# A transformer block on one core: value products, modulation sums, routing of expert 0 and the last experts rearranged

## The chip, the cores and the metric

The kernel runs on one core of one Trainium2 chip, written in Bass and Tile. The metric is the device time of one execution in microseconds; the time before is the median of three runs, 1007.59 us (1006.1 to 1008.08). Lower is better.

## What is computed

One encoder block over 1024 tokens of width 1024, all in 32-bit floats. The reference, cut to what matters here:

```
sh1, sc1, g1, sh2, sc2, g2 = split(silu(c) @ w_ada + b_ada, 6)     # modulation, six rows of 1024
h = rmsnorm(x, norm_mix_g) * (1 + sc1) + sh1
u_f, q, k, v = split(h @ w_in, [512, 1024, 1152])                   # 512 Fourier, 8 query heads, 2 key/value heads of 64
q, k = rmsnorm(q, q_norm_g), rmsnorm(k, k_norm_g)
y_f = fourier_mix(u_f, w_fourier, b_fourier)
y_a = windowed_gqa(q, k, v, rel_bias, sink)                         # 128-token blocks, window of +-128
x = x + g1 * (concat(y_f, y_a) @ w_out)
h2 = rmsnorm(x, norm_ffn_g) * (1 + sc2) + sh2
aff = softmax(h2 @ w_router)                                        # 16 experts
for each expert: the 128 tokens with the largest aff; x[token] += g2 * aff * (silu(t @ w_gate) * (t @ w_up)) @ w_down
```

## The kernel before, in words

The tokens are eight tiles of 128. The work has four stages that follow each other on TensorE.

**Mixing stage (lines 200 to 544).** Tiles 0 and 1 are projected together while w_in is split into a high and a low part (three products stand for one 32-bit product). In this part the order on every engine is the written one: `in_order` (line 132) chains each engine's instructions. Then a loop over tiles 2 to 7 takes each in two halves (`for m, (t, kc0)`, line 500). A half transposes and splits the next chunk (`chunk`, line 265: TensorE transposes, ScalarE evacuates with scale and bias and makes the high part, VectorE the low part) and runs four `project` steps of nine products each. At a tile's first half x of tile t+3 is loaded, that of t+1 is scaled on ScalarE (`scale_x`, line 228) and that of t+2 is normalised (`norm_x`, line 225: ScalarE squares, VectorE, a power on GpSimd). After each `project` step comes `bg_tick` (line 358). It moves on the key and query normalisations of finished tiles (`qknorm`, line 285, a generator whose `yield`s count ticks: squares and a power; two ticks later GpSimd's multiplications; some ticks later TensorE's key transposes, line 309) and the modulation rows (`ada_parts`, line 147: VectorE sums eight weighted rows for each of four parts, lines 121 and 123, TensorE sums over the partitions, line 181, VectorE adds a bias, GpSimd stores the row). At every second step the modulation generator is moved on once more (line 537). In this loop no order is pinned: the scheduler of the language orders each engine's instructions by its own estimate of when they are ready.

**Fourier and attention stage (lines 547 to 1026).** For each of 16 units (a tile and a key/value head) `front` makes logits and softmax, and `back` (line 706) transposes the probabilities of two or three key blocks (`flip_p`, ScalarE copies them to a tile pT, two buffers) and multiplies each block with its values (line 727: two products of 64 output rows, side by side in TensorE's columns, two records each). Before, `back` alternates: block b+1 is transposed, `tick` lets other work in, block b is multiplied. `tick` (line 958) hands out steps of a filler: the Fourier part for the first units, then `oproj` (line 760), the output projection, which also writes x2 (the residual), h2 (the normalised rows for the experts) and, through `tail` (line 829), the router's logits and `aff` of each tile. A sorter (`srt`) keeps the best affinities of the first six tiles sorted. The order is the scheduler's.

**Routing (lines 1030 to 1309).** For expert 0 `choose` (line 1138) settles quickly which tokens it takes: it counts, against the sorted best values of six tiles, the affinities of the last two tiles, finds the threshold and ranks. `gate_parts` (line 1106) splits affinities into three bf16 parts. `gather_a` makes one-hot rows from the ranks, `gather` (line 1245) sums token numbers and gates on TensorE (line 1250) and issues GpSimd's indirect load of the chosen rows from h2 in DRAM (line 1259). Then the rows are transposed (line 1306) into xf, and the first six weight units are multiplied as plain 32-bit products (line 1228). `cut_unit` splits a weight unit in two parts (ScalarE high, VectorE low). From `gather(0)` on TensorE, VectorE and GpSimd run in written order (line 1326).

**Experts (lines 1329 to 1357).** Sixteen experts, 192 weight units of 1 MB, streamed through 13 buffers; order pinned on all engines. `put` (line 1273) makes an expert's last products, scales the result by gate and g2 (ScalarE and then GpSimd; for expert 15 one VectorE step, line 1286) and scatters it with an indirect, accumulating DMA (line 1287). All experts write the result into one buffer, ys.

The handling of the last tile decides how the attention stage runs into the routing:

```
normed(slice(0, 512), cur)               # h2 = x2 * rs * G2 (line 805), then + sh2 (line 806)
yield from tail(t, 1)                    # flips of the second half, logits (line 837), aff
normed(slice(512, D), after["aff"])
```

## Time and profile before

| | before |
|---|---|
| median of three runs | 1007.59 us (1006.1 to 1008.08) |
| profiled execution | 1009.72 us |
| its span, first to last instruction | 1007.6 us |
| TensorE busy in it | 949.8 us (94%) |
| VectorE, ScalarE, GpSimd busy | 788.1, 627.8, 404.7 us |
| mean granted TensorE clock | 0.971 |
| mixing stage ends, first product of the experts | about 172 us, 429.54 us |

All times come from one profiled execution, counted from its first instruction. A line such as L309 is a line of the kernel; where a helper records the operation (L81 to L83 for the three products of a split one, L86 and L87 for the split), the tile's name tells which it is. PE is TensorE, DVE VectorE, ACT ScalarE, POOL GpSimd, SP the engine that issues most DMAs. A 32-bit product leaves two records on TensorE. An "idle before" stands with the instruction that ended it, and the arrow names what that one had waited for. The granted clock is a share of TensorE's full clock; it has two levels, 0.50 and 1.00, and a mean between them tells how a stretch divides.

### The profile page before, as it was taken

Reading aid. Unit: us, or ns where it says so; the run is one execution under the profiler, and the core shown is the slowest. Engines: PE = TensorE matmul, PEld = TensorE weight load, DVE = VectorE, ACT = ScalarE, POOL = GpSimd, SP = SyncE. Lnnn points to the kernel's source line nnn. Section 1 sums busy time; section 2 is a strip of 40 time slices with the busy share of each in tenths; the row PEclk is TensorE's granted clock in tenths of the full one; section 3 lists DMA queues with packets and bytes.
Section 4 is the critical chain, followed back from the end, with each engine's and each line's share of the span. In section 5 each row is a group of like instructions: output and inputs, shape, how many; then the busy total and the mean of one; then the engine's idle time right before and its main releaser. Section 6 shows DMA issues by size and latency. Waiting matters only on the chain.

```text
span 1007.6 us, 13138 instructions
## 1 busy us (share of the span) xinstructions
PE 949.8 (94%) x4737; PEld 747.4 (74%) x4737; DVE 788.1 (78%) x1240; ACT 627.8 (62%) x832; POOL 404.7 (40%) x236
## 2 busy tenths in 40 slices
PE   4997999979999999499899999999999999999995
PEld 2675877657777778358788888888888888888884
DVE  1346874787667787879869889988988898899894
ACT  2473533656555552136767777778777777777872
POOL 0025552200000000000257678769766976882203
PEclk9998999989999999599989999999999999999998
DMA  9967582461222228799989999999999999999912
GB/s 291 328 246 251 209 313 83 134 183 47 98 84 74 74 84 289 314 335 355 390 343 359 385 396 399 387 385 409 388 389 385 411 385 389 404 392 387 386 68 42
DMA packets 91641, 283.95 MB, mean 282 GB/s; under 512 B 8140, under 2 KB 25728, under 8 KB 91448
## 3 DMA queue, kind: packets, MB, share of 16 engines
q1 hardware_dynamic: 86712, 266.32, 69.5%
q0 software_dynamic: 4864, 16.80, 6.5%
q8 instruction: 37, 0.61, 0.2%
q14 instruction: 28, 0.23, 0.1%
HBM read 263.79 MB, written 21.40 MB: 283 GB/s over the span
## 4 chain that ended last, share of the span: by engine, by line
PE 83%; DVE 6%; POOL 3%; issue 2%; ACT 2%; DMA 1%; SPq 1%; POOLq 0%; ACTq 0%
PE pa L81 17%; PE pa L82 16%; PE pa L83 16%; PE pu L374 5%; PE yp L727 3%; PE pt L1269 3%; PE pj L81 2%; PE pj L82 2%; PE pt L714 2%; PE pj L83 2%; PE pa L1228 2%; PE pt L837 2%; PE lg L685 1%; DVE ws L123 1%; PE lg L686 1%
## 5 line engine op out<-in xcount | busy, mean ns | idle before, releaser
L87 DVE TENSOR_TENSOR wl<-raw,wh 128x2048 fp32r<-128x2048 f32 (+1 forms) x189 | 424.2, 2275 | 56.0 <-ACT wh L86 54.9
L86 ACT ACTIVATE wh<-raw 128x2048 fp32r<-128x2048 f32 (+1 forms) x189 | 355.4, 1896 | 73.7 <-PE pa L82 65.8
L1242 POOL TENSOR_SCALAR oneh<-tri_f,pos 128x128 bf16<-128x128 f32 x96 | 210.5, 2207 | 15.1 <-PE pt L1250 14.8
L81 PE MATMUL pa<-wh,t1h 128*128 128x512 f32 x384 | 151.4, 394 | 0.0
L83 PE MATMUL pa<-wl,t1h 128*128 128x512 f32 x384 | 149.5, 389 | 0.0
L82 PE MATMUL pa<-wh,t1l 128*128 128x512 f32 x384 | 149.5, 389 | 0.0
L81 PE MATMUL pa<-wh,t0h 128*128 128x512 f32 x360 | 143.5, 399 | 0.0
L82 PE MATMUL pa<-wh,t0l 128*128 128x512 f32 x360 | 141.1, 392 | 0.0
L83 PE MATMUL pa<-wl,t0h 128*128 128x512 f32 x360 | 141.1, 392 | 0.0
L800 POOL TENSOR_TENSOR rs<-ss,mhalf 128x1 f32<-128x1 f32 x8 | 4.5, 558 | 221.3 <-DVE ss L798 194.4
L1284 POOL TENSOR_TENSOR ys<-ys,g_r 128x512 f32<-128x512 f32 x30 | 54.5, 1837 | 84.9 <-ACT ys L1283 84.9
L83 PEld LDWEIGHTS pa<-wl,t1h 128*128 128x128 f32 x384 | 72.1, 188 | 15.1
L82 PEld LDWEIGHTS pa<-wh,t1l 128*128 128x128 f32 x384 | 72.2, 188 | 14.2
L81 PEld LDWEIGHTS pa<-wh,t1h 128*128 128x128 f32 x384 | 72.1, 188 | 14.2
L83 PEld LDWEIGHTS pa<-wl,t0h 128*128 128x128 f32 x360 | 68.1, 189 | 14.5
L81 PEld LDWEIGHTS pa<-wh,t0h 128*128 128x128 f32 x360 | 68.3, 190 | 13.7 <-issue 0.2
L82 PEld LDWEIGHTS pa<-wh,t0l 128*128 128x128 f32 x360 | 68.2, 190 | 13.6 <-issue 0.2
L1259 POOL DMA_INDIRECT xe<-h2d,idx x16 | 18.7, 1171 | 147.3 <-DVE gt L1256 147.2
L1287 POOL DMA_INDIRECT out_dram<-ys,idx x16 | 50.8, 3174 | 10.9 <-DVE ys L1286 6.4
L688 DVE CUSTOM_DVE_ANT_0 sb<-lg,bias,sink 128x384 f32<-128x384 f32 (+1 forms) x64 | 35.3, 579 | 17.4 <-PE pt L714 9.8
L278 ACT ACTIVATE hf<-pt,sh1c,G1c 128x128 f32<-128x128 f32 (+1 forms) x56 | 22.6, 480 | 38.7 <-PE pt L271 38.7
L374 PE MATMUL pu<-wh,hh 128*128 128x512 f32 x128 | 43.6, 423 | 2.3 <-ACT hh L86 2.2
(311 smaller groups left out, 1649.0 us busy)
## 6 DMA issues: line engine op xcount, KB each, us to landing
raw<-in_w_gate_dram SPq DMA_DIRECT2D x64, 1024.0 KB, 10.0
raw<-in_w_up_dram SPq DMA_DIRECT2D x64, 1024.0 KB, 8.5
raw<-in_w_down_dram SPq DMA_DIRECT2D x63, 1024.0 KB, 8.6
raw<-in_w_ada_dram SPq DMA_DIRECT2D x16, 1024.0 KB, 8.6
raw<-in_w_ada_dram SPq DMA_DIRECT2D x16, 512.0 KB, 8.7
xt<-in_x_dram SPq DMA_DIRECT2D x8, 512.0 KB, 5.0
raw<-in_w_out_dram SPq DMA_DIRECT2D x4, 1024.0 KB
raw<-in_x_dram SPq DMA_DIRECT2D x8, 512.0 KB
```

What stands on the lines that cost most here:

```text
L81: PE.matmul(o, lh, rh, start=start, stop=False)
L82: PE.matmul(o, ll, rh, start=False, stop=False)
L83: return PE.matmul(o, lh, rl, start=False, stop=stop)
L86: ACT.activation(hi, src, AF.Copy)
L87: return (eng or DVE).tensor_tensor(lo, src, hi.bitcast(F32), op=OP.subtract)
L374: PE.matmul(acc[:, :c1 - c0], lhs, r[kc][:, c0:c1], start=first, stop=(kc == 7 and r is w_l), skip_group_check=c0 == 1024)
L688: DVE.tensor_tensor_reduce(sb[:, :wid], lg[:, :wid], bias[:, kv * 4 + i, j0:j0 + wid], 1.0, sk[:, i:i + 1], op0=OP.add, op1=OP.max, accum_ ...
L727: PE.matmul(yp[par * 64:par * 64 + 64, :256], vf[:, b, kv * 64:kv * 64 + 64], pT[:, par * 256:par * 256 + 256], start=(bi == 0), stop=(bi ...
L1242: (POOL if t < shared else DVE).tensor_scalar(oneh[:, t, :], slots, pos[:, t, e:e + 1], None, op0=OP.is_equal)
L1269: PE.transpose(p[:, k * 128:k * 128 + 128], src[:, (4 * b + k) * 128:(4 * b + k + 1) * 128], ident)
L1284: POOL.tensor_tensor(ys[:, cs_], ys[:, cs_], g2_r[:, cs_], op=OP.mult)
L1287: POOL.indirect_dma_start(out=out2, out_offset=bass.IndirectOffsetOnAxis(ap=idx[:, :1], axis=0), in_=ys, in_offset=None, compute_op=OP.add)
```

## The change

Mixing stage: the loop's order is pinned on VectorE, ScalarE and GpSimd; x of tile 4 is loaded before the loop; the extra step of the modulation generator goes, so that its sums are spread over the whole loop; tile 1's normalisation starts four ticks later, and key transposes come six ticks after GpSimd's multiplications in place of four. Attention: all blocks of a unit are transposed first, and the value products then stand in one row; pT has three buffers, and one Fourier tile shares the buffer of the Fourier weights. Last tile: h2 is first made as x2 * G2 behind the residual, and then finished by one step per half, the first after aff, the second inside `choose(0)`; the first half's logits stand ahead of the second half's flips. Routing: the last two tiles' gate parts move to GpSimd, ahead of the choice; one equality count moves behind the threshold test; the indirect load is issued before the gate is summed; expert 1's choice and one-hot rows move ahead of the weight splits; the first rows are transposed in groups of 2, 2 and 4. Experts: the last two are scaled on VectorE, and expert 15 writes into the buffer hs in place of ys.

```diff
@@ -31,7 +31,7 @@
 SCRATCH = 4096
-SB, PB, WB, YB = 9, 2, 4, 3
+SB, PB, WB, YB = 9, 3, 4, 3
 OLD = NT - 2
@@ -283,6 +283,10 @@
     def qknorm(t, kk):
+        if t == 1:
+            for _ in range(4):
+                yield
         q_n = qn[t]
@@ -300,10 +304,8 @@
             POOL.tensor_tensor(kd[:, :, dup, :], kv_, gg[:, None, :].to_broadcast([128, 2, 64]), op=OP.mult)
-        yield
-        yield
-        yield
-        yield
+        for _ in range(6):
+            yield
         p = px_[0]()
@@ -459,6 +461,7 @@
     norm_x(3)
+    load_x(4)
     project(pair, 6, hs.pop(6), 0)
@@ -497,6 +500,7 @@
     seq = [(t, kc) for t in range(2, NT) for kc in (0, 4)]
+    t1 = traced()
     for m, (t, kc0) in enumerate(seq):
@@ -507,8 +511,6 @@
         if kc0 == 0:
-            if t == 2:
-                load_x(4)
             if t + 3 < NT:
@@ -533,14 +535,13 @@
                 level0(a)
-            if m > 0 and a % 2:
-                next(ada[0], None)
         if kc0 == 4:
...
         next(g)
+    in_order(t1, "DVE", "Activation", "Pool")
     p_a.close()
@@ -561,7 +562,7 @@
         SP.dma_start(cs, t_in["k_cs"].rearrange("a p c -> p a c"))
-        wf = pf.tile([128, 4, 128], F32, name="wf")
+        wf = pf.tile([128, 4, 128], F32, name="wf", tag="wf", bufs=1)
         POOL.memset(wf, 0.0)
@@ -592,7 +593,7 @@
             ACT.activation(AB[:, i], p.rearrange("p (a b) -> p a b", b=128), AF.Copy)
-        p2 = [pf.tile([128, 2, 256], F32, name=f"p2{i}") for i in range(2)]
+        p2 = [pf.tile([128, 2, 256], F32, name=f"p2{i}", tag=("wf", "p2")[i], bufs=1) for i in range(2)]
         for o in p2:
@@ -716,16 +717,16 @@
-        nxt = flip_p(0)
+        pTs = []
+        for bi in range(len(blocks)):
+            pTs.append(flip_p(bi))
+            yield
+            tick()
         for bi, b in enumerate(blocks):
-            yield
-            pT = nxt
-            if bi + 1 < len(blocks):
-                nxt = flip_p(bi + 1)
-            tick()
             for par in range(2):
                 PE.matmul(yp[par * 64:par * 64 + 64, :256], vf[:, b, kv * 64:kv * 64 + 64],
-                          pT[:, par * 256:par * 256 + 256], start=(bi == 0), stop=(bi == len(blocks) - 1))
+                          pTs[bi][:, par * 256:par * 256 + 256], start=(bi == 0), stop=(bi == len(blocks) - 1))
         ypv = yp[:, :256].rearrange("p (a b) -> p a b", b=128)
@@ -789,6 +790,8 @@
             lastadd = DVE.tensor_tensor(x2[:, cs_], x2[:, cs_], h2[:, cs_], op=OP.add)
+            if t == NT - 1:
+                DVE.tensor_tensor(h2[:, cs_], x2[:, cs_], G2_r[:, cs_], op=OP.mult)
             junk = at0.tile([128, 512], BF, name="junk", tag="qn1")
@@ -808,9 +811,14 @@
                 drain(srt)
-            normed(slice(0, 512), cur)
             yield from tail(t, 1)
-            normed(slice(512, D), after["aff"])
+            def scaled(c, prev):
+                with tc.issue_after(prev.ins):
+                    DVE.scalar_tensor_tensor(h2[:, c], h2[:, c], rs, sh2_r[:, c], op0=OP.mult, op1=OP.add)
+            scaled(slice(0, 512), after["aff"])
+            after["kept"] = lambda kept: scaled(slice(512, D), kept)
         else:
@@ -828,12 +836,17 @@
         x2, rs = x2s.pop(t)
+        p = None
         for b in range(b0, 2):
+            if b0:
+                p = pt()
+                for kc in range(4):
+                    PE.matmul(p[:, :16], x2Ts[t][:, kc, :], wrG[:, kc, :], start=(kc == 0), stop=False)
             x2_flip(t, b, x2)
...
         x2T = x2Ts.pop(t)
-        p = pt()
-        for kc in range(8):
+        p = p or pt()
+        for kc in range(4 * b0, 8):
             PE.matmul(p[:, :16], x2T[:, kc, :], wrG[:, kc, :], start=(kc == 0), stop=(kc == 7))
@@ -1103,12 +1116,12 @@
-    def gate_parts(a, b):
-        DVE.tensor_copy(aux[:, a:b, :, 2], aff[:, a:b])
-        DVE.tensor_tensor(r1[:, a:b], aff[:, a:b], aux[:, a:b, :, 2], op=OP.subtract)
-        DVE.tensor_copy(aux[:, a:b, :, 3], r1[:, a:b])
-        DVE.tensor_tensor(r1[:, a:b], r1[:, a:b], aux[:, a:b, :, 3], op=OP.subtract)
-        DVE.tensor_copy(aux[:, a:b, :, 4], r1[:, a:b])
+    def gate_parts(a, b, eng):
+        eng.tensor_copy(aux[:, a:b, :, 2], aff[:, a:b])
+        eng.tensor_tensor(r1[:, a:b], aff[:, a:b], aux[:, a:b, :, 2], op=OP.subtract)
+        eng.tensor_copy(aux[:, a:b, :, 3], r1[:, a:b])
+        eng.tensor_tensor(r1[:, a:b], r1[:, a:b], aux[:, a:b, :, 3], op=OP.subtract)
+        eng.tensor_copy(aux[:, a:b, :, 4], r1[:, a:b])
@@ -1131,7 +1144,7 @@
         DVE.tensor_tensor(gq[:, :nt], aff[:, :nt, es], th, op=OP.is_gt)
-        DVE.tensor_tensor(gq[:, nt:], aff[:, :nt, es], th, op=OP.is_equal)
+        after["gq"] = DVE.tensor_tensor(gq[:, nt:], aff[:, :nt, es], th, op=OP.is_equal)
         return gq
@@ -1150,6 +1163,7 @@
         k0 = DVE.tensor_scalar(kept, acc[:, 0:1], rank0, 127.0, op0=OP.add, op1=OP.is_le)
+        after.pop("kept", lambda kept: None)(k0)
         with tc.issue_after(k0.ins):
@@ -1157,16 +1171,21 @@
         e0 = DVE.scalar_tensor_tensor(edge, pn[:, :1], rank1, best[:, e:e + 1], op0=OP.is_equal, op1=OP.mult)
+        def equal(a, val, w, wid):
+            junk = rt.tile([128, 256], BF, name="junk", bufs=2)
+            DVE.scalar_tensor_tensor(junk[:, :wid], p[:, :wid], val, w, op0=OP.is_equal, op1=OP.mult,
+                                     accum_out=acc[:, a:a + 1])
         with tc.issue_after(e0.ins):
             above(3, v7)
-            for a, val, w, wid in ((2, v6, below, 128), (4, v7, both, 256)):
-                junk = rt.tile([128, 256], BF, name="junk", bufs=2)
-                DVE.scalar_tensor_tensor(junk[:, :wid], p[:, :wid], val, w, op0=OP.is_equal, op1=OP.mult,
-                                         accum_out=acc[:, a:a + 1])
+            equal(2, v6, below, 128)
         yield
...
         gq = at_least(pe[:, :1], OLD, slice(e, e + 1))
+        with tc.issue_after(after["gq"].ins):
+            equal(4, v7, both, 256)
         yield
@@ -1198,15 +1217,17 @@
-    gate_parts(0, OLD)
+    gate_parts(0, OLD, DVE)
     for m in LATER:
...
     tsp = traced()
+    gate_parts(OLD, NT, POOL)
+    c0 = choose(0)
+    next(c0)
     SP.dma_start(h2d[rows, :], h2)
     SP.dma_start(out2[rows, :], x2)
-    drain(choose(0))
-    gate_parts(OLD, NT)
+    drain(c0)
@@ -1250,14 +1271,14 @@
         DVE.tensor_scalar(idx, p[:, 0:1], p[:, 1:2], None, op0=OP.add)
+        xe = wk.tile([128, D], F32, name="xe", bufs=1)
+        after["p"] = POOL.indirect_dma_start(out=xe, out_offset=None, in_=h2d,
+                                in_offset=bass.IndirectOffsetOnAxis(ap=idx[:, :1], axis=0))
         ax = wk.tile([128, 6], F32, name="ax", bufs=2)
...
         after["v"] = DVE.tensor_tensor(gt[:, 1:2], gt[:, 0:1], ax[:, 2:3], op=OP.add)
-        xe = wk.tile([128, D], F32, name="xe", bufs=1)
-        after["p"] = POOL.indirect_dma_start(out=xe, out_offset=None, in_=h2d,
-                                in_offset=bass.IndirectOffsetOnAxis(ap=idx[:, :1], axis=0))
         gs[e] = idx, gt[:, 1:2], xe
@@ -1276,10 +1297,10 @@
         idx, gate, _ = gs[e]
-        ys = wk.tile([128, D], F32, name="ys", bufs=1)
+        ys = wk.tile([128, D], F32, name="ys" if e < NE - 1 else "hs", bufs=1)
         for hf in range(2):
             cs_ = slice(hf * 512, hf * 512 + 512)
-            if e < NE - 1:
+            if e < NE - 2:
                 ACT.activation(ys[:, cs_], o[hf], AF.Copy, scale=gate)
@@ -1293,19 +1314,16 @@
     SP.dma_start(g2_r, md[3:4, :].to_broadcast([128, D]))
+    drain(choose(1))
+    oneh = gather_a(1)
     cut_unit(2)
-    c1 = choose(1)
-    next(c1)
-    next(c1)
     cut_unit(2)
-    drain(c1)
     xf = wk.tile([128, D], F32, name="ys", bufs=1).rearrange("p (k c) -> p k c", c=128)
-    for b in range(2):
+    for k0, n in ((0, 2), (2, 2), (4, 4)):
         p = pt()
-        for k in range(4):
-            PE.transpose(p[:, k * 128:k * 128 + 128], gs[0][2][:, (4 * b + k) * 128:(4 * b + k + 1) * 128], ident)
-        ACT.activation(xf[:, 4 * b:4 * b + 4], p.rearrange("p (a b) -> p a b", b=128), AF.Copy)
-    oneh = gather_a(1)
+        for k in range(n):
+            PE.transpose(p[:, k * 128:k * 128 + 128], gs[0][2][:, (k0 + k) * 128:(k0 + k + 1) * 128], ident)
+        ACT.activation(xf[:, k0:k0 + n], p[:, :n * 128].rearrange("p (a b) -> p a b", b=128), AF.Copy)
     xh, xl = (wk.tile([128, 8, 128], F32R, name=f"t0{x}", bufs=1) for x in "hl")
```

## Rows read from the trace of the kernel before

**Rows 1.** Waits of TensorE: who waited for whom, us in total, times, longest.

```profile
PE pt L309 <- ACT hf L278: 6.2, 1, 6.2
...
PE pt L1250 <- DVE t1l L87: 3.6, 1, 3.6
```

**Rows 2.** Windows: length, busy time (instructions) of each engine, granted clock, DMA share, GB/s.

```profile
91.40:96.40 5.00, 4.99 (x14) 3.39 (x16) 2.08 (x4) 1.45 (x4) 0.00 (x0) 0.50 0.89 364
...
100.00:116.30 16.30, 16.20 (x87) 12.90 (x86) 13.43 (x16) 8.28 (x19) 10.14 (x11) 1.00 0.50 183
...
223.00:404.00 181.00, 180.60 (x1024) 133.31 (x1023) 135.14 (x472) 97.68 (x268) 4.53 (x9) 0.99 0.30 108
...
404.40:429.50 25.10, 12.13 (x75) 9.94 (x74) 21.18 (x90) 4.07 (x8) 2.36 (x3) 0.55 0.80 314
...
425.00:450.00 25.00, 22.56 (x75) 11.18 (x75) 19.36 (x74) 8.22 (x8) 0.96 (x1) 0.88 0.92 343
```

**Rows 3.** Timeline of GpSimd and ScalarE, 86 to 88 us: start, length, operation.

```profile
86.13 1.53 POOL L196 TENSOR_TENSOR xr<-xs,mhalf 128x1 f32<-128x1 f32 x1
...
87.70 1.15 ACT L229 ACTIVATE xt<-xt,xr 128x1024 f32<-128x1024 f32 x1 [8.79 <-POOL xr L196]
```

**Rows 4.** The instructions of line L123: count, duration min/median/max, first and last start.

```profile
L123 DVE SCALAR_TENSOR_TENSOR ws<-raw,c_act,ws x28: 1269/1285/1418, 75.8 to 141.7; 128x1024 f32<-128x1024 f32 x28
```

**Rows 5.** Timeline of TensorE in the attention stage.

```profile
249.85 0.40 PE L82 MATMUL pj<-woh,yl 128*128 128x512 f32 x1
250.08 0.40 PE L83 MATMUL pj<-wol,yh 128*128 128x512 f32 x1
250.41 0.65 PE L727 MATMUL yp<-pT,vf 128*64 128x256 f32 x4
250.99 0.66 PE L714 MATMUL pt<-ident,sb 128*128 128x128 f32 x4
...
375.09 1.08 PE L727 MATMUL yp<-pT,vf 128*64 128x256 f32 x8
```

**Rows 6.** Windows of line L727 alone: PE and PEld busy (records), clock, DMA.

```profile
223.00:404.00 181.00, 29.49 (x168) 8.97 (x168) 0.99 0.30 108
```

**Rows 7.** Timeline of TensorE in the routing.

```profile
407.33 3.43 PE L837 MATMUL pt<-wrG,x2T 128*128 128x16 f32 x16
...
427.75 1.95 PE L1306 MATMUL pt<-ident,xe 128*128 128x128 f32 x8
429.54 2.63 PE L1228 MATMUL pa<-raw,ys 128*128 128x512 f32 x4
```

**Rows 8.** Timeline of ScalarE in the routing.

```profile
407.57 0.60 ACT L827 ACTIVATE x2T<-pt 128x512 f32<-128x512 f32 x1
```

**Rows 9.** Timeline of VectorE in the routing.

```profile
410.95 0.68 DVE L806 TENSOR_TENSOR raw<-raw,sh_r 128x512 f32<-128x512 f32 x1
...
413.91 0.69 DVE L806 TENSOR_TENSOR raw<-raw,sh_r 128x512 f32<-128x512 f32 x1
...
415.84 0.48 DVE L1164 SCALAR_TENSOR_TENSOR junk<-pt,aff,tri_f 128x256 bf16<-128x256 f32 x1
...
419.76 0.22 DVE L1252 TENSOR_SCALAR idx<-pt 128x1 int32<-128x1 f32 x1 [0.28 <-PE pt L1250]
...
420.36 2.35 DVE L87 TENSOR_TENSOR wl<-raw,wh 128x1024 fp32r<-128x1024 f32 x2
```

**Rows 10.** Timeline of GpSimd in the routing.

```profile
420.83 1.72 POOL L1259 DMA_INDIRECT xe<-h2d,idx  x1 [11.98 <-DVE gt L1256]
```

**Rows 11.** DMA issues, 420 to 424 us: operation, count, median us to landing.

```profile
xe<-h2d,idx POOLq DMA_INDIRECT x1, 5.0
```

**Rows 12.** Timeline of VectorE at the end.

```profile
988.19 4.10 DVE L87 TENSOR_TENSOR wl<-raw,wh 128x1024 fp32r<-128x1024 f32 x2 [0.37 <-ACT wh L86]
998.27 1.41 DVE L1286 SCALAR_TENSOR_TENSOR ys<-pa,gt,g_r 128x512 f32<-128x512 f32 x2 [5.98 <-DMA out_dram<-ys,idx]
```

**Rows 13.** Timeline of TensorE at the end.

```profile
996.97 0.39 PE L83 MATMUL pa<-wl,t1h 128*128 128x512 f32 x1
```

## The prediction

> **What bounds the kernel now.** I read the waits of TensorE first, then windows around the longest of them, then the timelines of the engines that end them, and last the tail. TensorE sets the pace: in the attention and output-projection stretch it is busy 180.60 of 181 us [rows 2], so a microsecond taken out of its own work there is a microsecond off the span, while VectorE, ScalarE and GpSimd matter only where TensorE stands still. It stands still in few places. The longest wait is 6.2 us in the projection loop, before a key transpose (L309); another is 3.6 us at L1250 [rows 1]. The routing stretch from 404.40 to 429.50 has TensorE busy 12.13 of 25.10 us at a mean granted clock of 0.55 [rows 2]: there a chain that hops between TensorE, VectorE, ScalarE and GpSimd sets the time. After the 6.2 us wait the granted clock is 0.50, the lower of its two levels (1.2 GHz), for 5.00 us in which TensorE is busy 4.99 [rows 2], so that work took about 2.5 us longer than at full clock.
>
> **Mixing loop: spread sums, earlier load, pinned order.** The 6.2 us wait ends with ScalarE's chunk evacuation, but ScalarE had itself sat 8.79 us idle until the scaling of tile 4's x at 87.70, and that waited for GpSimd's power for tile 4, run at 86.13 behind the key and query normalisation of tiles 0 and 1 [rows 3]. The change attacks this in three ways: tile 4's x is loaded before the loop (one 512 KB load, ahead of the bias and norm-gain loads and the first w_ada fetches on SP), so that in the written order, now pinned, its power stands ahead of that normalisation; tile 1's normalisation starts four ticks later; and transposes come two ticks later. All 6.2 us can go, and with the wait the half-clock stretch: 6.2 + 2.5 = 8.7 us. What is late next is the modulation sums. There are 28 accumulating steps of 1.285 us (median) [rows 4], plus one plain first step in each of four parts. They now come one per tick instead of one and a half, so VectorE has less per tile: it was busy 13.43 us in a 16.30 us stretch as long as a tile [rows 2], and two steps fewer make about 10.9. But VectorE, ScalarE and GpSimd now run strictly in written order, so VectorE stands still at each chunk's split until ScalarE is through, and TensorE's four column sums (L181) may meet a late accumulator. I set 1.2 us aside for them, a step's length, and take 7.5. Bounds: 0 (another wait takes its place) to 8.7. The shared buffer of the Fourier weights and one spread tile costs nothing: the first write into the tile already follows the products that read the weights. The load costs nothing either, since the loop reads tile 4 only two tiles later; were that cover gone, ScalarE's wait would stay and with it the whole term.
>
> **Value products in one row.** An output-projection product takes 0.23 us from start to start (249.85 to 250.08); the one before a group of value products takes 0.33 (to 250.41), and the group of four records (two products) 0.58 (to 250.99): 0.10 + 0.58 = 0.68 us. A group of eight records that happens to run in one row is 1.08 us long, where four are 0.65, so a block added to a row costs 0.43 [rows 5]. Each merge saves 0.25 us. There are 168 records in this stretch [rows 6], 42 groups, and the 15 units left here become 15 rows: 27 merges, 6.7 us. TensorE's order isn't pinned here, and a product whose operand is ready early may be issued before the others, so I count three quarters, 5.1; bounds 1.5 to 6.7. The third pT buffer only lets the three blocks of a row live together.
>
> **Routing chain.** (a) The 16 records of the last tile's logits run from 407.33 for 3.43 us, 0.214 each [rows 7]. The first eight now run in the idle time before the last flips; the second eight need the copy that ends at 408.17 [rows 8] and end 1.71 later, at 409.9 in place of 410.8: 0.9. (b) The addition at 410.95 (0.68) leaves the path between logits and maximum: 0.5. (c) That at 413.91 (0.69) leaves the path to expert 0's first count: 0.6. (d) In their place one scaled step follows that count, ahead of the edge: -0.7. (e) The equality count at 415.84 (0.48) moves behind the threshold test: 0.35, as a product of TensorE runs under part of it [rows 9]. (f) Five small gate steps leave VectorE's end of the chain: 0.2. On GpSimd they take between 1.1 (0.22 each, as the index step) and 7.7 us (1.53 each, as the power in [rows 3]); they have some 4 us of cover, and beyond it the gather waits, 3.5 at worst. Sum of (a) to (f): 1.85. (g) GpSimd's gather starts at 420.83 [rows 10], 0.85 after the index was ready at 419.98 [rows 9]; issued ahead of the gate's three steps it gains 0.4. The stores of the last rows lie behind weight loads on SP's queue and could hold it; then (g) gains nothing. (h) The rows land 5.0 us later [rows 11], at 425.8, but their transposes start at 427.75 [rows 7], because expert 1's choice stands ahead of them on TensorE and waits for weight splits on VectorE. The change puts that choice and its one-hot rows ahead of the splits: 1.95. Transposes in groups of 2, 2 and 4 still all precede the first product (1.8 us at 429.54 [rows 7]): nothing. Sum: 4.2. The splits, two units of 2.35 us [rows 9], now run beside the first products; VectorE has 5.6 of 25 us free from 425 to 450 [rows 2]. Were that gone, the wait at L1250 would grow by up to 4.7. Bounds: 0.5 to 6.
>
> Here a rule of the Trainium skill speaks against the change: "GPSIMD Engine Reference", § 8 Key points, says that GpSimd shares its SBUF interfaces with VectorE and contends with instructions of two SBUF inputs. The rows agree: two half-unit splits took 4.10 us at the end, beside GpSimd's multiplications, and 2.35 alone [rows 9, 12]. By that rule the scaled step of (d), run beside the gate steps, would take 1.2 and not 0.7 us, and the sum would be 0.5 smaller.
>
> **Last two experts.** VectorE's last scaling starts at 998.27, after 5.98 us idle, when the scatter of expert 14 has released the buffer, and takes 1.41 [rows 12]. The last product starts at 996.97 and is 0.39 long [rows 13]. With its own buffer the first half is scaled earlier and the second ends at 997.4 + 0.7 = 998.1 in place of 999.7: 1.5 us. The two scalings of expert 14 stand ahead of the last splits, which ended at 992.29; their products begin 12 steps of 0.23 before the end, at 994.6, so 1.4 us more is covered. Bounds: 0 to 1.6.
>
> **Sum.** 7.5 + 5.1 + 4.2 + 1.5 = 18.3 us. The profiled execution took 1009.72 us (span 1007.6), 2.1 above the median of the three runs, 1007.59; so 991.4 for it, and 989.3 for the median. The expert loop is untouched; its wait at L1250 stays.
>
> **Rivals.** (1) The mixing wait only moves: TensorE waits for the running sums or the keys instead. For it: three engines in fixed order, with no slack where written order is bad. Against: VectorE loses two steps per tile. Gain 10.8: 996.8. (2) The change doesn't do what it says in attention: the products are issued as soon as each is ready, no rows form, or VectorE and ScalarE set the pace there. For it: the unpinned order. Against: groups of eight do occur [rows 5]. The products give 0 to 1.5, so about 993.5. (3) Slower: in the mixing loop the pinned order makes VectorE and ScalarE take turns. Per tile ScalarE has 8.28 us of work [rows 2]; wholly in series with VectorE's 10.9 to 13.43 that is 19.2 to 21.7 us against 16.3, 17 to 32 us over six tiles, less the 8.7 and the other terms' 10.8. From 3.25 us per tile unhidden it decides; in its middle, 24.5, 1012.6. Against: VectorE can run ahead of TensorE on the sums, which need no product.
>
> **How the numbers follow.** Forecast 0.60, rival 1 0.16, rival 2 0.13, rival 3 0.07, and 0.04 that pieces of several cancel. About 0.2% (2 us) is what a measurement of this kernel can tell from no change. Forecast and rivals 1 and 2 are all faster: 0.89; rival 3 is mostly slower, and half of the rest: 0.08; same 0.03. The upper bounds sum to 23, or 984.6; rival 1 with a small loss elsewhere reaches 999. Range 984 to 999.5.
>
> **What would show it.** Right: no wait above 1 us at L309 and clock 1.00 around it; TensorE records of value products in groups of 8 and 12; eight logit records before the last flips; the transposes of expert 0's rows starting at their landing; a last scaling under 0.8 us after the last product. Wrong: new waits on L181 or a chunk's split; value products still in fours; the gather held by a DMA; a longer wait at L1250.

## The result and the profile after

The changed kernel takes **994.39 us** (median of 5 runs, 993.94 to 995.88) against 1007.59 us (5 runs, 1004.64 to 1011.92): ratio 0.9862, 95% interval 0.984 to 0.9884. Forecast were 989.3 us and the range 984 to 999.5. The profiled execution took 994.39 us with a span of 992.1; that of before stood 2.1 us above its median, so from profile to profile the span lost 15.5 us where 18.3 were forecast.

Cut at the same instructions in both traces, the 15.5 us lie here:

| Stretch, from and to (TensorE) | before, us | after, us | difference | forecast |
|---|---|---|---|---|
| mixing loop: first transposes of tile 2 to first Fourier product | 111.09 | 105.56 | -5.53 | -7.5 |
| Fourier part, to the first low-part product of the output projection (L82) | 46.36 | 45.63 | -0.73 | 0 |
| attention and output projection, to the last tile's flips | 187.12 | 180.70 | -6.42 | -5.1 |
| routing, to the first expert product | 22.87 | 21.24 | -1.63 | -4.2 |
| expert loop, to the last product | 567.43 | 567.81 | +0.38 | 0 |
| end, to the end of the span | 10.63 | 9.03 | -1.60 | -1.5 |

Three waits of TensorE after (who waited for whom, us in total, times, longest; answers to [rows 1]):

```profile
PE pt L1325 <- DMA xe<-h2d,idx: 4.0, 1, 4.0
PE pt L1271 <- DVE t1l L87: 3.6, 1, 3.6
PE pt L181 <- DVE ws L123: 2.9, 2, 1.7
```

The key transposes' 6.2 us are gone. The wait at L1271 is that of L1250 before, as long as it was. New are 2.9 us at the modulation's column sums (two waits, 1.25 and 1.69 us), 2.6 more than before (0.38), and 4.0 us on a DMA: the gathered rows of expert 0.

The same windows as in [rows 2], shifted to the stretches after (length, busy time of each engine, granted clock, DMA share, GB/s):

```profile
89.50:96.40 6.90, 6.90 (x37) 5.03 (x36) 4.38 (x6) 0.68 (x2) 6.07 (x6) 1.00 0.76 262
100.00:116.30 16.30, 15.05 (x78) 11.90 (x77) 13.50 (x16) 7.78 (x18) 9.49 (x8) 1.00 0.59 199
213.30:394.00 180.70, 178.78 (x1041) 138.99 (x1042) 139.25 (x483) 100.31 (x273) 4.47 (x9) 0.98 0.33 119
394.00:415.30 21.30, 10.06 (x67) 7.42 (x68) 19.03 (x86) 2.44 (x7) 4.18 (x8) 0.56 0.70 274
```

Around 90 us the clock is now full (0.50 before). In the second line TensorE is busy 15.05 of 16.30 us: the 1.25 us wait at a column sum lies there. The attention stretch is still TensorE's, busy 178.78 of 180.70, and the routing still runs at about half clock.

**Value products.** TensorE's timeline (start, length, operation) shows a whole row of three blocks (answers to [rows 5]):

```profile
247.31 1.51 PE L728 MATMUL yp<-pT,vf 128*64 128x256 f32 x12
```

Twelve records in 1.51 us: 0.43 for each block after the first, as forecast. Counted over the stretch, the 168 records stand in 18 groups (ten of 12, four of 8, four of 4), where before they stood in 44.

**Routing.** GpSimd, VectorE, and TensorE after, one fence each (answers to [rows 7, 9, 10, 11]):

```profile
408.71 1.12 POOL L1275 DMA_INDIRECT xe<-h2d,idx  x1 [7.42 <-DVE gq L1147]
```

```profile
405.45 0.22 DVE L1273 TENSOR_SCALAR idx<-pt 128x1 int32<-128x1 f32 x1 [0.28 <-PE pt L1271]
```

```profile
394.02 0.63 PE L834 MATMUL pt<-ident,raw 128*128 128x128 f32 x4 [1.01 <-DVE raw L792]
413.18 2.28 PE L1325 MATMUL pt<-ident,xe 128*128 128x128 f32 x8 [3.98 <-DMA xe<-h2d,idx]
415.26 3.10 PE L1249 MATMUL pa<-raw,ys 128*128 128x512 f32 x5
```

The index is ready at 405.67 and the gather goes out only at 408.71, 3.04 us later. The releaser named in brackets, a comparison of VectorE (L1147), had ended by 402.3, so it was something else, and the experiments find it: the store of the last rows, which SP issued behind five 1 MB weight loads, the last of which this fence shows (timeline of SP's queue):

```profile
392.84 0.47 SPq L1076 DMA_DIRECT2D raw<-in_w_gate_dram  x1
400.85 0.34 SPq L1228 DMA_DIRECT2D h2d<-raw  x1
```

**End.** VectorE after (answers to [rows 12]); the last product starts at 983.07:

```profile
975.15 2.35 DVE L87 TENSOR_TENSOR wl<-raw,wh 128x1024 fp32r<-128x1024 f32 x2
983.50 0.75 DVE L1307 SCALAR_TENSOR_TENSOR hs<-pa,gt,g_r 128x512 f32<-128x512 f32 x1 [0.61 <-PE pa L83]
```

The last scaling ends 1.18 us after the start of the last product (2.71 before), and the last splits take 2.35 us. They took 4.10 before, and 4.09 in the run below that changes only the buffer at the end, where GpSimd still multiplies beside them.

### The profile page after: what moved, and what is told of

The parts are those of the page before. It is cut to its first block, busy times and chain, and to the rows that moved or that the text cites. A ratio compares the mean times of both kernels' runs of the same rounds, so it can differ in the third digit from the quotient of the medians.

```text
span 992.1 us, 13155 instructions
## 1 busy us (share of the span) xinstructions
PE 938.7 (95%) x4737; PEld 745.1 (75%) x4737; DVE 788.6 (79%) x1237; ACT 626.2 (63%) x831; POOL 403.3 (41%) x239
## 4 chain that ended last, share of the span: by engine, by line
PE 56%; DMA 1%; DVE 1%; issue 0%; POOLq 0%; ACT 0%; DVEq 0%
PE pa L81 17%; PE pa L83 17%; PE pa L82 17%; PE pt L1290 3%; PE pa L1249 2%; DMA out_dram<-ys,idx 1%; DMA xe<-h2d,idx 0%; DVE wl L87 0%; PE pt L1271 0%; PE pt L1325 0%; POOLq L1439 0%; DVE oneh L1263 0%; DVE ys L1307 0%; PE pa L1135 0%; DVE t1l L87 0%
## 5 line engine op out<-in xcount | busy, mean ns | idle before, releaser
L87 DVE TENSOR_TENSOR wl<-raw,wh 128x2048 fp32r<-128x2048 f32 (+1 forms) x189 | 422.4, 2266 | 55.8 <-ACT wh L86 54.8
L82 PE MATMUL pa<-wh,t1l 128*128 128x512 f32 x384 | 149.5, 389 | 0.0
L82 PE MATMUL pa<-wh,t0l 128*128 128x512 f32 x360 | 141.2, 392 | 0.0
L82 PEld LDWEIGHTS pa<-wh,t1l 128*128 128x128 f32 x384 | 72.2, 188 | 14.3
L82 PEld LDWEIGHTS pa<-wh,t0l 128*128 128x128 f32 x360 | 68.3, 190 | 13.8 <-issue 0.2
L1305 POOL TENSOR_TENSOR ys<-ys,g_r 128x512 f32<-128x512 f32 x28 | 50.0, 1802 | 46.1 <-ACT ys L1304 46.1
L717 ACT ACTIVATE pT<-pt 128x512 f32<-128x512 f32 x44 | 25.9, 596 | 30.9 <-PE pt L715 30.8
```

Of the source, the lines that this page charges most:

```text
L82: PE.matmul(o, ll, rh, start=False, stop=False)
L87: return (eng or DVE).tensor_tensor(lo, src, hi.bitcast(F32), op=OP.subtract)
L717: ACT.activation(pT, pp, AF.Copy)
L1305: POOL.tensor_tensor(ys[:, cs_], ys[:, cs_], g2_r[:, cs_], op=OP.mult)
```

## The experiments

Stretches are named as in the table. Six profiles with the mixing loop as the change has it give 105.53 to 105.63 us for it, so with that order a difference of half a microsecond can be read; how far the unpinned loop varies from profile to profile was not measured.

### Mixing: which part took the 6.2 us away

**Without the pin** (changed kernel):

```diff
-    in_order(t1, "DVE", "Activation", "Pool")
```

> The changed kernel (994.39 us) without the pinned order of VectorE, ScalarE and GpSimd in the mixing loop; the earlier load, the spread sums and the delayed normalisation stay. Theory, as in the prediction: the pin is what keeps tile 4's power ahead of the normalisation of tiles 0 and 1 on GpSimd, so without it a wait of 3 to 6.2 us at the key transposes comes back, with half clock behind it: 998 to 1003 us. Rival: the earlier load alone puts the power early, and the pin only makes the accumulators of the column sums late (waits of 2.9, 2.0 and 1.7 us at L181): those waits go, the key wait stays away, 989 to 992 us.

995.51 us (ratio 0.9883, 0.9865 to 0.99), mixing loop 106.12 us. Neither theory holds whole: the key wait stays away and so do VectorE's late sums at L181, as the rival said, but the time doesn't fall. ScalarE's timeline shows what does come back, the idle time of [rows 3]:

```profile
86.86 1.15 ACT L229 ACTIVATE xt<-xt,xr 128x1024 f32<-128x1024 f32 x1 [8.80 <-POOL xr L196]
```

and TensorE's, that it now costs 0.80 and 1.97 us, and half clock from 94.1 to 97.5:

```profile
90.48 1.05 PE L181 MATMUL pt<-ws,ones 128*32 128x512 f32 x4 [0.80 <-ACT hf L278]
93.50 0.65 PE L271 MATMUL pt<-ident,xt 128*128 128x128 f32 x4 [1.97 <-DVE klo L87]
```

Counting the scalings (L229) shows that this one is tile 5's, not tile 4's: the six busy ones start at 60.9, 62.0, 70.2, 87.7, 106.7 and 121.6 before, for tiles 2 to 7. With the pin, in the changed kernel, ScalarE scales tile 4 at 83.81 and tile 5 only at 100.43, while GpSimd's power for tile 5 runs at 86.35, when it ran before (86.13):

```profile
83.81 1.16 ACT L229 ACTIVATE xt<-xt,xr 128x1024 f32<-128x1024 f32 x1
100.43 1.17 ACT L229 ACTIVATE xt<-xt,xr 128x1024 f32<-128x1024 f32 x1
```

```profile
86.35 0.56 POOL L196 TENSOR_TENSOR xr<-xs,mhalf 128x1 f32<-128x1 f32 x1 [0.29 <-DVE xs L194]
```

So the pin does not bring the power forward; it puts the scaling that waits for it a tile later on ScalarE, behind the chunk evacuation that TensorE needs.

**The early load alone** (kernel before):

```diff
     norm_x(3)
+    load_x(4)
...
-            if t == 2:
-                load_x(4)
```

> The kernel before (1007.59 us) with one edit: tile 4's x is loaded ahead of the mixing loop, as in the change; no pin, no spread sums, no delayed normalisation. Theory, after the run without the pin: the early load is what takes the 6.2 us wait at the key transposes away, since with it the power for tile 4 can run before the normalisation of tiles 0 and 1: 6 to 8.7 us less, 999 to 1002 us. Rival: the load is not what was late (GpSimd is taken by the normalisation whenever the load lands), and the delay of tile 1's normalisation or the spread sums did it: 1006 to 1009 us with the wait of about 6 us still there.

1007.77 us (ratio 1.0004, 0.9987 to 1.002): nothing that the time shows, as the rival said. TensorE's wait at L309 is 6.18 us, as it was, and GpSimd's power for tile 5 starts at 85.92, behind the same normalisation.

**The pin alone** (kernel before):

```diff
     for g in bg[-1:]:
         next(g)
+    in_order(t1, "DVE", "Activation", "Pool")
```

> The kernel before (1007.59 us) with the pinned order of VectorE, ScalarE and GpSimd in the mixing loop and nothing else of the change. Theory, from the run without the pin, where ScalarE still sat 8.8 us idle ahead of tile 5's scaling: the pin takes that idle time away, since the scaling, written a tile later, no longer stands ahead of the chunk evacuation on ScalarE; the 6.2 us wait and the half clock behind it go, but the sums, still one and a half a tick, come late at L181 and at the chunks: 999 to 1004 us. Rival (the prediction's slower case): with the old spacing the three engines take turns and the new waits exceed the old one: 1008 to 1020 us.

1016.51 us (ratio 1.009, 1.0057 to 1.0123), slower by some 9 us. Waits of TensorE from 60 to 179 us:

```profile
PE pt L309 <- POOL kd L302: 6.0, 3, 5.0
PE pu L374 <- DVE hl L87: 3.7, 2, 3.4
PE pt L309 <- ACT hf L278: 1.9, 1, 1.9
```

The old wait on ScalarE falls to 1.9 us, and two others take its place: key transposes that come before GpSimd has the keys, and products whose split VectorE has not reached. The mixing loop takes 118.40 us. So the pinned order can cost more than it gains, as the prediction's slower rival feared, though the longest wait is not VectorE and ScalarE in turns but TensorE waiting for GpSimd's keys; the rest of the change keeps it from deciding.

**The delays alone** (kernel before):

```diff
     def qknorm(t, kk):
+        if t == 1:
+            for _ in range(4):
+                yield
...
-        yield
-        yield
-        yield
-        yield
+        for _ in range(6):
+            yield
```

> The kernel before with the later normalisation of tile 1 (four ticks) and the later key transposes (two ticks) and nothing else of the change. Theory: in the run without the pin TensorE's 6.2 us wait was down to 0.8 and 2.0 us although ScalarE was idle as long as before, so it is these delays that hide it, by leaving products ahead of the transposes: 1.5 to 5 us less, 1002.5 to 1006 us, ScalarE's idle time of about 8.8 us still there. Rival: without fewer sums on VectorE the cover is gone, the wait stays near 6 us: 1006 to 1009 us.

1006.56 us (ratio 0.999, 0.9972 to 1.0008): not told apart from no change by the time. In the profile the mixing loop takes 108.97 us, 2.1 less. The first wait is down to 1.1 us, but VectorE's arrears make two others (waits from 60 to 179 us):

```profile
PE pt L271 <- DVE ws L183: 3.1, 1, 3.1
PE pt L181 <- DVE ws L123: 2.4, 3, 1.7
PE pt L311 <- ACT hf L278: 1.1, 1, 1.1
```

**The spread sums alone, and in the same kernel the last expert's buffer alone** (kernel before):

```diff
-            if m > 0 and a % 2:
-                next(ada[0], None)
...
-        ys = wk.tile([128, D], F32, name="ys", bufs=1)
+        ys = wk.tile([128, D], F32, name="ys" if e < NE - 1 else "hs", bufs=1)
```

> The kernel before with two edits in stages 800 us apart, read apart in the profile: the modulation sums one step a tick in place of one and a half (no delay, no pin, no early load), and a buffer of its own for the last expert's scaled rows, with expert 14 still scaled on ScalarE and GpSimd. Mixing, from the first transposes of the loop's tiles to the first Fourier product, 111.1 us before and 105.6 after the change; the delays alone gave 109.0, the load alone 110.4, all but the pin 106.1. Theory: the 6.2 us wait comes from the key transposes standing early, which the spread does not touch, so it stays near 6 us and the stretch takes 109.5 to 111: the delays take the first wait away and the spread the one that VectorE's backlog then makes. Rival: VectorE's sums were the whole cause: 106 to 108 us, wait gone. End, from the start of the last product to the end of the span, 10.6 us before and 9.0 after: theory: the buffer alone gives 8.9 to 9.2, since the last scaling waited for nothing else; rival: expert 14's slower scaling and scatter still hold the last scatter, 10 us or more. Time in all: 1004 to 1007 us by the theories, 1001 to 1004 by the first rival.

1007.35 us (ratio 0.9986, 0.9973 to 0.9999). Mixing goes as the theory said: 110.25 us, and the wait is there:

```profile
PE pt L309 <- ACT hf L278: 6.1, 1, 6.1
```

Put together, the mixing loop against 111.09 us before, one profile each: load alone -0.7, spread alone -0.8, delays alone -2.1, pin alone +7.3, all but the pin -5.0, all four -5.5. The parts do not add. The delays take the key wait away, but alone they leave VectorE late; with the spread sums and the load these waits are gone. The pin pays only on top of the other three, and then 0.5 us. Delays and spread without the load were not run together, so what the load does beside them is not shown.

The end lies between its two theories, 9.84 us. GpSimd's timeline there shows why:

```profile
990.07 2.24 POOL L1285 DMA_INDIRECT out_dram<-ys,idx  x1 [0.28 <-POOL ys L1282]
997.89 1.55 POOL L1285 DMA_INDIRECT out_dram<-hs,idx  x1 [5.58 <-DMA out_dram<-ys,idx]
```

The last rows are scaled at 996.74, but their scatter waits until 997.89 for expert 14's scatter to land. From profile to profile the end varies: 10.62 to 11.11 us in four with the old end, 9.03 to 9.44 in nine with the new one. So the buffer is worth 0.8 to 1.3 us, and VectorE's quicker scaling of expert 14, which sends that scatter out earlier (7.56 us ahead of the last product and not 5.49), 0.4 to 0.8.

**The late accumulators.** Two edits of the changed kernel, one tick more ahead of the column sum, and, with the same number of ticks, each accumulating step a tick earlier:

```diff
             yield
+            yield
             p = pt()
```

> The changed kernel with each of the four column sums of the modulation (L181) written one tick later. Theory: the accumulator is late by 1.2 to 1.7 us there only because VectorE does its sums in written order just ahead of the column sum; one tick (2.1 us) more takes three waits of 2.9, 2.0 and 1.7 us away: 988 to 991 us, and the end of the mixing moves from 167.7 to 162 to 165. Rival: VectorE as a whole is behind in the loop, so the same lateness shows at the next split or transposes: 993.5 to 995.5 us, L181 gone from the list of waits but the end of the mixing unmoved.

996.79 us (ratio 0.9897, 0.9878 to 0.9916), mixing loop 106.75 us. The waits at the column sum grow to 4.6 us, 3.0 of them at the last one: the four extra ticks don't fit before the last chunk, where the rest is run off at once. (The change has two waits there, not the three that the expectation names.)

```diff
                 for j in range(2):
-                    yield
                     mac(acc, u[:, j:j + 1], 1, 2 * q + j)
+                    yield
```

> The changed kernel with the accumulating steps of the modulation written one tick earlier each (the same ticks in all; the column sum L181 so stands two ticks behind its last step, not one). Theory: VectorE in written order reaches the last step too late only by being given it one tick ahead of the column sum; waits of 2.9 us in all at L181 go and nothing takes their place: 990.5 to 992.5 us. Rival, which the run with more ticks speaks for: VectorE is behind by a whole chunk in the loop, and the wait comes back at L181 or at the next chunk's split: 993.5 to 996 us.

994.25 us (ratio 0.9862, 0.9836 to 0.9888). The waits fall only from 2.9 to 2.5 us, the mixing loop to 104.65, and from its start to the first output projection it is 152.45 us, as in the run with the held loads (152.42): what was gained is given back in the Fourier part, which had a granted clock of 0.90 here and 0.96 there. A tick is not what makes the sums late.

### Attention: what a row is worth

**Alternating again** (changed kernel, with the `back` of before):

```diff
-        for bi in range(len(blocks)):
-            pTs.append(flip_p(bi))
-            yield
-            tick()
         for bi, b in enumerate(blocks):
+            yield
+            pT = nxt
+            if bi + 1 < len(blocks):
+                nxt = flip_p(bi + 1)
+            tick()
```

> The changed kernel with the value products again written one block after each flip, not in one row. Theory: the 24 groups that merged (44 to 20) are worth 0.25 us each, so the stretch from the first product of the first Fourier rows to the last tile's flips grows by 4.5 to 6 us: 999 to 1001 us. Rival: most of the 6.4 us that the stretch lost came from a wait and a half-clock dip that went by chance, and the rows are worth 1 to 2 us: 995 to 996.5 us.

999.99 us (ratio 0.9928, 0.991 to 0.9947): the theory. The records stand in 44 groups again. The window of the attention stretch with alternating products, and then that of a run that keeps the rows (store first, below) and has its clock alike:

```profile
213.30:399.60 186.30, 183.90 (x1042) 136.71 (x1042) 140.31 (x489) 100.59 (x273) 4.52 (x9) 0.99 0.33 118
```

```profile
213.30:393.10 179.80, 177.83 (x1041) 138.52 (x1041) 139.27 (x483) 100.37 (x272) 4.49 (x9) 0.99 0.33 118
```

The rows are worth 6.5 us of this stretch, 6.07 of them TensorE's busy time: 26 groups fewer at 0.23 us, against the 0.25 a merge of the prediction. Part of it is given back at once: with alternating products the routing took 18.87 us, with rows 21.24. With the same short chain the gather went out 0.85 us after its index there (ready at 411.16; GpSimd's timeline), and not 3.04:

```profile
412.01 1.12 POOL L1276 DMA_INDIRECT xe<-h2d,idx  x1 [5.22 <-DMA out_dram<-raw]
```

The loads and stores on SP's queue had run off some 11 us after the last flips there, and with rows some 13 us after them: a shorter attention stage brings the flips nearer to loads that are still queued.

### Routing: what holds the gather

**Store first** (changed kernel): the last three of the late loads go behind the store.

```diff
-    for m in LATER:
+    for m in LATER[:2]:
         load(m)
...
     SP.dma_start(out2[rows, :], x2)
+    for m in LATER[2:]:
+        load(m)
```

> The changed kernel with the last three of the five late 1 MB weight loads issued on SP behind the store of the last normalised rows and not ahead of it. Theory: the gather of expert 0's rows stood 3.0 us after its index was ready because the store lay behind 8 MB of loads; with the store ahead of 3 MB the gather is issued near 406 instead of 408.71, the first product at 412.5 to 413.5 instead of 415.26: 991.5 to 993 us. Rival: the gather now shares the DMA engines with the three loads and lands as late as before, or the products wait for the fifth and sixth weight block: 994 to 996 us.

995.21 us (ratio 0.9878, 0.986 to 0.9896): the rival. The gather does go out early, 0.85 us after its index, as before the change (GpSimd's timeline, then the DMA issues of that stretch with us to landing):

```profile
405.78 1.12 POOL L1277 DMA_INDIRECT xe<-h2d,idx  x1 [5.21 <-DVE gt L1283]
```

```profile
xe<-h2d,idx POOLq DMA_INDIRECT x1, 7.5
```

But its rows land 7.5 us after that, at 413.28: 20.1 us after the flips, where it was 19.1 without the edit. The DMA queues from 405.7 to 410 us, and from 410 to 413 (packets, MB, share of 16 engines; q0 is the gather's, q1 SP's):

```profile
q1 hardware_dynamic: 397, 1.54, 92.0%
```

```profile
q1 hardware_dynamic: 191, 0.73, 60.2%
q0 software_dynamic: 144, 0.52, 42.9%
```

For these 4.3 us not one packet of the gather runs, and then the two queues share the engines. The Trainium skill ("DMA: Bandwidth & Descriptors", Queues, rings and completion order) says that each DMA engine takes turns between its queues packet by packet. The second window fits that, 144 packets to 191; the first it does not explain, and no run here does.

**Gather first** (changed kernel): the same three loads wait until GpSimd has issued the gather, by the means that held unit 11 back (a small GpSimd write into the buffer).

```diff
-EARLY, LATER, HELD = (6, 7, 2, 3, 9, 10), (0, 1, 4, 5, 8), 11
+EARLY, LATER, HELD = (6, 7, 2, 3, 9, 10), (0, 1), 4
```

> The changed kernel with three of the 1 MB weight loads (units 4, 5 and 8) held until GpSimd has issued the gather of expert 0's rows. With those loads right behind the store, the gather was issued 2.9 us earlier but its rows landed 7.5 us after issue instead of 4.4. Theory: what holds the gather is the DMA engines' backlog, first through the store and then through its own packets; with nothing queued at its issue near 406 it lands in about 4.4 us, near 410.5, and the first product starts at 412 to 413 instead of 415.3: 991 to 992.5 us. Rival: the later loads are needed as early as the gather was (products of units 4 to 8 wait for them), or the 3 us come back at the next wait: 994 to 997 us.

992.16 us (991.51 to 993.13; ratio 0.9851, 0.9827 to 0.9875): the theory. Timeline of GpSimd, then of TensorE:

```profile
405.49 1.12 POOL L1275 DMA_INDIRECT xe<-h2d,idx  x1 [5.21 <-DVE gt L1281]
```

```profile
392.86 0.63 PE L834 MATMUL pt<-ident,raw 128*128 128x128 f32 x4 [1.01 <-DVE raw L792]
409.99 2.28 PE L1325 MATMUL pt<-ident,xe 128*128 128x128 f32 x8 [1.82 <-DVE oneh L1263]
412.06 4.77 PE L1249 MATMUL pa<-raw,ys 128*128 128x512 f32 x8
```

From flips to first product 19.20 us, 2.04 less than the change and 3.67 less than before. The step lengths of the four kernels:

| | before | after | store first | gather first |
|---|---|---|---|---|
| flips to index ready | 13.31 | 11.65 | 11.78 | 11.78 |
| index to gather issued | 0.85 | 3.04 | 0.85 | 0.85 |
| gather to rows landed | 5.0 | 4.4 | 7.5 | 4.5 |
| landed to transposes | 1.92 | 0.07 | 0.04 | 0.0 |
| transposes to first product | 1.79 | 2.08 | 2.07 | 2.07 |

### The expert loop's wait, which the change left alone

**Later** (changed kernel):

```diff
             o = gather_a(e)
-            yield from wait(7)
+            yield from wait(7 if e == 2 else 13)
             gather(e, o)
```

> The changed kernel with expert 3's gather product written six steps of the background list later (some two products, past the transposes of expert 1's hidden rows). Theory: the 3.6 us wait at that product, which the change left alone, comes only from its bank: the transposes just ahead of it fill both banks of that kind and their splits lie behind two weight splits on VectorE. Two products later the banks are free: 3.6 us of wait and some 3 us of half clock behind it go: 987.5 to 990.5 us. Rival: the wait moves to the next user of the banks, or to the products whose splits then come later: 993 to 995.5 us.

1000.83 us (ratio 0.9936, 0.9912 to 0.996), 6.4 us slower than the change: neither theory. The 3.6 us wait goes, and a longer one comes at the transposes of the gathered rows (TensorE, then GpSimd):

```profile
521.10 1.94 PE L1290 MATMUL pt<-ident,xe 128*128 128x128 f32 x8 [10.31 <-DMA xe<-h2d,idx]
```

```profile
491.75 19.30 POOL L1263 TENSOR_SCALAR oneh<-tri_f,pos 128x128 bf16<-128x128 f32 x8 [16.46 <-PE pt L1271]
511.21 2.66 POOL L1275 DMA_INDIRECT xe<-h2d,idx  x1 [0.16 <-issue]
```

Expert 3's gather is queued on GpSimd behind expert 4's one-hot rows, which took 19.30 us here and 6.82 in the same place after the change.

**Earlier, with the gather first** (changed kernel with the three loads held as above):

```diff
-            while step[0] < 12 * e - 16:
+            while step[0] < (8, 19)[e - 2]:
                 yield
```

> The changed kernel with three weight loads held behind expert 0's gather, as in the run that gave 992.16 us, and expert 3's one-hot rows and gather product one product earlier, ahead of the transposes of expert 1's hidden rows that fill both banks (six background steps later it cost 6 us, since GpSimd issued the gather behind expert 4's one-hot rows and the rows came 10 us late). Theory: the product finds its bank free and waits at most for its one-hot rows, under 1 us; 3.6 us of wait and the half clock behind it (6.8 us in which work takes some 3 us longer) go: 985.5 to 989 us. Rival: the one-hot rows stand ahead of the product of the hidden rows on VectorE, the transposes wait instead, and the same time is lost: 991 to 993 us.

**987.95 us** (6 runs, 986.55 to 988.78; ratio 0.9802, 0.9777 to 0.9827): faster than both kernels, 6.4 us below the change and 4.2 below the run with the gather first alone. TensorE's timeline, and its window, with the clock full throughout:

```profile
481.97 0.35 PE L1271 MATMUL pt<-aux,oneh 128*128 128x6 bf16 x8
486.55 0.66 PE L1290 MATMUL pt<-ident,hs 128*128 128x128 f32 x4 [0.94 <-DVE ax L1278]
```

```profile
480.00:500.00 20.00, 19.06 (x96) 15.52 (x95) 19.51 (x20) 13.78 (x9) 15.54 (x9) 1.00 1.02 389
```

The product finds a free bank and waits for nothing; 0.94 us come back at the second half of the transposes. The expert loop takes 563.22 us, 4.6 less than after the change and 5.1 less than with the gather first alone (568.36). There the same place ran at half clock after its 3.6 us wait:

```profile
488.50:495.30 6.80, 5.51 (x21) 4.35 (x21) 4.57 (x8) 0.42 (x2) 5.04 (x5) 0.50 0.99 368
```

## Why the prediction came out as it did

The sign, the stretches and the range were right. Between the two profiles the sum was 2.8 us too large, 18.3 against 15.5. The median forecast, 989.3, missed by 5.1: it took off the 2.1 us by which the profile before stood above its median, as if the profile after would stand as far above its own, and that one stands on it. Mixing and routing gave 4.5 us less than forecast, attention and the Fourier part 2.0 more; that these offset each other in part is luck. Step by step:

- **Mixing, 7.5 forecast, 5.5 measured.** That the wait and the half clock go was right: the wait was 6.18 us, and TensorE's busy time in the loop fell from 103.52 to 101.53 us, so the half clock was worth 2.0 and not 2.5. The term set aside for column sums was the right place but too small: 2.6 us of new waits at L181 where 1.2 were set aside. In true size the terms are 6.2 + 2.0 - 2.6 = 5.6. The cover given for them, "VectorE loses two steps per tile", was about half there: in 16.3 us some 5.8 of the 28 accumulating steps run and not 6.8, and in the stretch from 100.00 to 116.30 us VectorE is busy 13.50 us, as before (13.43), not 10.9. The steps after (answer to [rows 4]):

```profile
L123 DVE SCALAR_TENSOR_TENSOR ws<-raw,c_act,ws x28: 1268/1285/2341, 78.7 to 155.7; 128x1024 f32<-128x1024 f32 x28
```

 The mechanism failed at one step, "in the written order, now pinned, its power stands ahead of that normalisation". The scaling that waited was tile 5's; its power runs when it ran before. "The change attacks this in three ways" fell too: the early load alone shows nothing in the time, and the pin alone costs some 9 us. The delays and the spread sums, with the load beside them, do most of the work (-5.0), more than their parts alone (-3.6). "The load costs nothing" holds.
- **Value products, 5.1 forecast, 6.4 in the table, 6.5 by the experiment.** The price of a merge, 0.25 us, was right (0.23). The discount of a quarter was not needed: 26 merges formed, from 44 groups to 18, where 27 were counted, from 42 to 15.
- **Routing, 4.2 forecast, 1.6 measured.** (a) to (f), 1.85, came out at 1.66; (h), 1.95, at 1.85. The step that failed is (g): "issued ahead of the gate's three steps it gains 0.4", with nothing as the worse case. It lost 2.2. The text named the store behind the weight loads, but bounded its effect at no gain. The index was ready 1.66 us sooner after the flips and the store landed later after them (SP's queue had run off some 13 us after the last flips, 11.4 before), mostly since the rows had shortened the attention stage; the prediction added these terms as if one did not touch the other. The rest is the gather, which landed 0.6 us quicker, and the transposes to the first product, 0.3 us longer. With the loads out of the way the term is 3.67, near the forecast.
- **The rule weighed in (d).** VectorE's scaled step took 0.74 us at 400.08, beside GpSimd's gate steps, near the 0.68 it was taken at, not 1.2. GpSimd's step with two inputs beside it took 0.83 us; its twin, beside a count of VectorE that reads one of its inputs from PSUM (L1161), took 0.26 (VectorE, then GpSimd):

```profile
400.08 0.74 DVE L818 SCALAR_TENSOR_TENSOR raw<-raw,rs,sh_r 128x512 f32<-128x512 f32 x1
```

```profile
399.42 0.26 POOL L1121 TENSOR_TENSOR r<-aff,aux 128x32 f32<-128x32 f32 x1
...
400.11 0.83 POOL L1123 TENSOR_TENSOR r<-r,aux 128x32 f32<-128x32 f32 x1
```

 The Trainium skill's rule ("GPSIMD Engine Reference", § 8 Key points), that the two contend for SBUF interfaces, fits these rows, but here it was GpSimd that paid, off the path.
- **End, 1.5 forecast, 1.6 measured**, for a part of the reason given: the buffer is worth 0.8 to 1.3, expert 14's earlier scatter the rest.
- **The rivals.** The first (the mixing wait only moves) held in part, 2.9 us at L181. The second (no rows form) did not. The third, a pinned order that costs more than it gains, is what the pin does alone, at 7.3 us of the mixing loop and not the 17 to 32 of wholly serial work, and by waits for GpSimd's keys more than by engines in turns; the other three edits keep it away. The Fourier part's 0.7 us are no part of the change: it takes 45.6 us in two and 46.8 to 46.9 in four profiles with the same code, by where the half clock falls (granted clock 0.99 in the two, 0.96 in the four).

## What to carry to other kernels

When a chain of small steps ends in a gather, look at what its DMA must wait for, a store and the packets queued ahead of it, before you shorten the chain: loads that nobody needs yet go behind the gather's issue, not only behind the store. Find out which instruction an idle engine waits for by counting instances of its line, since a trace that leaves buffer numbers out will not say which tile it is. And test the parts of a scheduling edit alone and together: here four parts, worth between -2 and +7 us each, made -5.5 together. Ask too what a gain in one stage does to the next: here the shorter attention stage ran into loads still queued.

## What was not expected of the hardware

- **GpSimd's steps took longer, the more of VectorE's weight splits ran beside them.** The eight one-hot rows of expert 4 (128x128 each) took 6.82 us after the change, 12.87 in the fastest kernel and 19.30 in the one with the late gather, the same eight instructions. VectorE's splits (L87, two inputs) filled 2.40 of the first 6.8 us, 11.27 of the second 12.9 (the weight splits alone 10.15; the others read a PSUM tile) and 16.70 of the last 19.3. Three lengths show the order, not the size of the effect. The windows of that line alone (length, VectorE's busy time, clock, DMA share, GB/s), after and with the late gather:

```profile
490.30:497.10 6.80, 2.40 (x3) 0.63 0.99 373
```

```profile
491.80:511.10 19.30, 16.70 (x9) 1.00 1.00 374
```

- **A gather's start.** With nothing queued, the first packet ran 0.70 us after GpSimd's issuing step had ended. From the start of the step that is 1.82 us in the changed kernel and in the run with the gather first, where the step took 1.12 us, and 2.42 us in the kernel before, where it took 1.72 beside a split on VectorE. Behind a filled queue of SP it came after 4.27 us, and landing went from 4.5 to 7.5 us.
- **The half clock falls on the same instructions in one profile and not in another.** From 31 to 34.6 us the profile of the changed kernel ran at 0.53, and that of the run with the store first at 1.00, with TensorE busy all the time in both; of the 14 profiles four are at 0.53 to 0.57 there and ten at 1.00. From the first product after 30 us (30.11 and 30.49) to the loop's first transposes (62.13 and 60.95) the one took 32.02 us and the other 30.46. The windows, first after, then store first:

```profile
31.00:34.60 3.60, 3.60 (x12) 2.89 (x11) 0.88 (x4) 0.22 (x1) 0.00 (x0) 0.53 1.09 347
```

```profile
31.00:34.60 3.60, 3.60 (x21) 2.98 (x20) 1.26 (x4) 0.67 (x2) 0.00 (x0) 1.00 1.09 347
```

 A difference of a microsecond between two profiles is no evidence until the clock has been compared.
